# Slot rows of the MoE compared from broadcast places instead of transposed one-hot rows, with the mixers' tails reordered

## The chip, the cores and the metric

The kernel runs on one core of a Trainium2 chip. The metric is the device time of one execution in microseconds (us), the median of several runs. The engines are PE (TensorE; PEld is its weight load), DVE (VectorE), ACT (ScalarE), POOL (GpSimd) and SP (SyncE, which here only issues DMAs).

## The reference

Two layers on one sequence of 256 tokens, 1024 wide, all in float32:

```python
for l in range(2):
    sh1, sc1, g1, sh2, sc2, g2 = split(silu(c) @ ada_w[l] + ada_b[l], 6)
    h = rmsnorm(x, norm_mix_g[l]) * (1 + sc1) + sh1
    pa, pb, pc = split(h @ w_in[l])            # three head groups A, B, C
    mix = concat(oa, ob, oc) @ w_out[l]        # A differential, B sliding window with sinks, C dilated
    x = x + g1 * mix
    h = rmsnorm(x, norm_ffn_g[l]) * (1 + sc2) + sh2
    # router: best of 4 groups, then 2 of its 4 experts, gates sum to the group's weight
    y = sum over 16 experts e: gate[:, e] * ((silu(h @ w_gate[e]) * (h @ w_up[e])) @ w_down[e])
    x = x + g2 * y
return rmsnorm(x, final_norm_g)
```

## The kernel before, in words

Tokens lie on the 128 partitions in two tiles t = 0, 1. All weights, 283 MB, pass once through on-chip memory: SP issues their loads one after the other in a fixed order (`Ring.load`, L154) into a ring of 29 tiles of 512 KB (`big`), with tiles of the pools `k` and `w` lent to it now and then. A tile is loaded again only when its last reader (a PE matmul, or the DVE that splits it) has finished; when SP reaches such a load too early it waits, and every load behind it with it.

PE runs in the order in which the program is written. The orders of DVE, ACT and POOL are set by a scheduler when the kernel is built, and each engine then runs its own list strictly from front to back.

**The mixer** of a layer is written as a list of steps, `MIX`, which ends in `TAIL`. `P..` are the pieces of the input projection and `W.` those of the output projection; weights are split into two fp32r parts for them (cast on ACT, L776; subtraction on DVE, L781) and three matmuls made of each (L724 to L726). `AT, BT, CT` transpose a head group's queries and keys (L809, copies at L1074 on ACT and L1075 on DVE for group C). `AF, BF, CF` make scores (L1081) into one bank of the two-buffer PSUM pool `s` for each half of the heads, read them on DVE (L835, masked maximum, then nm at L839) and take exponentials on ACT (L841). `BV, CV` transpose the probabilities (L809) and copy them out (L866, ACT). Letters `a`, `c`, `d` are chunks of the adaLN products (a: L462, d: L537; a `d` is half of the 16 matmuls that the trace shows for two). Behind each `W` and `P`, `flush` runs work put off until then: among it `ada_columns` (L480), four transposes that turn adaLN rows into columns.

**The MoE** takes the experts in eight pairs j. Each token that chose an expert has a place in it, at most 64 of them, and `pos[:, t, e]` is that place plus one, or 0. One-hot matrices `hot` (tokens by slots) gather the rows of a pair. For the way back the kernel needs the transposed matrix, slots by tokens: `places(j)` makes it. Before pair 0 stand a chain of gates on POOL (L1279 to L1301) and, after the pair's gate products (L1372), `g2` (L568, copied out at L571 and L573). Pair 0's products `up` follow `places(0)` on PE.

Of the kernel before, what the change touches and what calls it, by code (L numbers as in the profile page):

```python
# [17 lines left out]
DEPTH = 2  # L18
# [19 lines left out]

_COLUMNS = (("ID", 128), ("C", KT), ("COLS", (6 * DEPTH + 2 * DEPTH) * KT), ("FREQ", 48), ("PAIR", 2), ("ADD", 2 * DEPTH), ("Z", 128), ("CAUSAL", 128),
            ("CFAR", 128), ("CDIAG", 128), ("IOTA", 64), ("LOW", 16), ("RANK", 4), ("ONES", 1),  # L40
            ("SEL", 20), ("SUBG", DEPTH * 64), ("SINK", DEPTH * 8), ("WR", DEPTH * KT * 20), ("RB", DEPTH * 20),
            ("BAND", 128), ("CAUSAL2", 128))
_AT, NCONST = {}, 0
for _name, _n in _COLUMNS:
# [11 lines left out]

START = ["X c c R c c S00".split(), "S00 S01 X0 X1 a S02 X2 a X3 a a R a".split()]
TAIL = """
CT0 d CT1 d d CF0 AM1 d W0 CF1
BV0 BV1 W1 BV2 BV3 BO0 BV4 W2 BV5 CV0 W3 BO1 CV1 CV2 W4 CO0 W5 W6  # L60
"""
MIX = [("""
P00 c P01 c P10 c c N P11 P02 P03 a a P12 L AT0 P13 a a AT1
P20 AF0 P21 a AF1 P22 a AF2 P23 a a
P30 AV0 P31 AV1 a AO0 BT0 P32 AV2 BT1 AO1 G2 P33 AO2 BF0 a a
P40 P41 BF1 a P42 AM0 P43 BF2 a a a H2 a
""" + TAIL).split(), ("""
P00 P01 P02 P03 P10 P11 AT0 P12 AT1 P13 AF0
P20 AF1 P21 a AF2 P22 P23
P30 AV0 P31 AV1 a AO0 BT0 P32 AV2 BT1 AO1 P33 AO2 BF0 a  # L70
P40 P41 BF1 P42 G2 AM0 P43 BF2 H2
""" + TAIL).split()]


# [6 lines left out]
def laid_out(inputs):  # L81


    t = {n: np.asarray(a) for n, a in inputs.items()}
    i = np.arange(128)[:, None]
    j = np.arange(128)[None, :]
    blob = np.zeros((128, NCONST), np.float32)
    blob[:, _AT["ID"]] = i == j
    blob[:, _AT["CAUSAL"]] = np.where(i >= j, 0.0, -BIG)
    blob[:, _AT["BAND"]] = np.where(j > i, 0.0, -BIG)  # L90

    def mixture(dist):
        n = (((dist >= 0) & (dist <= 128)).astype(int) + ((dist >= 0) & (dist % 4 == 0))
             + ((dist >= 0) & (dist % 16 == 0)))
        return np.where(n > 0, 8.0 * np.log(np.maximum(n, 1)), -BIG)

    blob[:, _AT["CFAR"]] = mixture(128 + i - j)
    blob[:, _AT["CDIAG"]] = mixture(i - j)
    blob[:, _AT["IOTA"]] = np.arange(1, 65)
    blob[:, _AT["LOW"]] = (np.arange(4)[:, None] > np.arange(4)[None, :]).reshape(16)  # L100
    blob[:, _AT["RANK"]] = [3, 2, 1, 0]
    freq = blob[:, _AT["FREQ"]]
    freq[:, 0:32] = (10000.0 ** (-np.arange(0, 64, 2) / 64)).astype(np.float32)
    freq[:, 32:48] = (10000.0 ** (-np.arange(0, 32, 2) / 32)).astype(np.float32)
    blob[:, _AT["ONES"]] = 1.0
    blob[:, _AT["PAIR"]] = i % 64 == 32 * np.arange(2)
    lh = np.arange(2 * DEPTH)
    blob[:, _AT["ADD"]] = (i == 64 + 32 * (lh % 2) + lh // 2) | (i == 32 * (lh % 2) + DEPTH)
    blob[:, _AT["SEL"]] = i % 32 == np.arange(20)
    blob[:, _AT["C"]] = by_partition(t["c"])  # L110
    blob[:, _AT["COLS"]] = by_partition(np.concatenate(
        [t["ada_b"].reshape(6 * DEPTH, D), t["norm_mix_g"], t["norm_ffn_g"]]))
    blob[:, _AT["SUBG"]] = t["diff_subln_g"].reshape(1, -1)
    blob[:, _AT["SINK"]] = t["swa_sinks"].reshape(1, -1)
    wr = np.concatenate([t["router_group_w"], t["router_expert_w"]], axis=2).reshape(DEPTH, KT, 128, 20)
    blob[:, _AT["WR"]] = wr.transpose(2, 0, 1, 3).reshape(128, -1)
    blob[:, _AT["RB"]] = np.concatenate([t["router_group_b"], t["router_expert_b"]], axis=1).reshape(1, -1)
    out = {"first": blob[:, :_AT["Z"].start], "rest": blob[:, _AT["CAUSAL"].start:_AT["CAUSAL2"].start]}
    out["x"] = t["x"]
    out["positions"] = t["positions"].reshape(2, 128).T  # L120
    out["lambdas"] = np.stack([t["diff_lambda_" + n] for n in ("q1", "k1", "q2", "k2")]).reshape(1, -1)
    out["final_norm_g"] = t["final_norm_g"]
    w = t["ada_w"][0, :, :2 * D].reshape(KT, 128, 2, 2, 512)
    out["ada_w_first"] = w.transpose(3, 0, 1, 2, 4).reshape(2, KT, 128, 1024)
    out["ada_w"] = t["ada_w"].reshape(DEPTH, KT, 128, 6 * D)
    w = t["w_in"].reshape(DEPTH, 4, 2, 128, 2304)
    out["w_in"] = w[..., :2048].reshape(DEPTH, 4, 2, 128, 4, 512).transpose(0, 4, 1, 3, 2, 5).reshape(DEPTH, 4, 4, 128, 1024)
    out["w_in_last"] = w[..., 2048:].transpose(0, 1, 3, 2, 4).reshape(DEPTH, 4, 128, 512)
# [71 lines left out]
class Body:  # L200
# [60 lines left out]
    def tables(self, posi):  # L261
        nc, const, cb = self.nc, self.const, self.cb

        posf = const.tile([128, 2], F32, name="posf")
        nc.vector.tensor_copy(posf, posi)
        ang = self.w()[:, 0:96].rearrange("p (t f) -> p t f", t=2)
        for t in range(2):
# [33 lines left out]
    def more_tables(self):  # L301
        nc, const, cb = self.nc, self.const, self.cb
        for l in range(DEPTH):
            nc.vector.tensor_scalar(self.subg[:, l], self.subg[:, l], 1.0 - self.lambda_init(l), None, op0=OP.mult)
        self.sink8 = const.tile([128, DEPTH, 8], F32, name="sink8")
        nc.vector.tensor_scalar(self.sink8, self.sink, 8.0, None, op0=OP.mult)
        self.trib = const.tile([128, 128], BF16, name="trib")
        nc.vector.tensor_scalar(self.trib, cb[:, C_CAUSAL:C_CAUSAL + 128], 0.0, None, op0=OP.is_lt)
        oneb = const.tile([128, 1], BF16, name="oneb")
        nc.vector.tensor_copy(oneb, cb[:, C_ONES:C_ONES + 1])  # L310
        self.oneb = oneb.to_broadcast([128, 128])
        self.ovf = const.tile([128, DEPTH], F32, name="ovf")

        self.beats = const.tile([128, 10, 4, 5], F32, name="beats")
        nc.gpsimd.tensor_copy(self.beats[:, :, :, 4],
                              cb[:, C_RANK:C_RANK + 4].unsqueeze(1).to_broadcast([128, 10, 4]))
# [138 lines left out]
    def ada_unit(self, l, q, i):  # L455
        nc = self.nc
        if i == 0:
            self.q = self.acc.tile([128, 512], F32, name="acc")
        keys = [("ada", l, v, i) for v in (2 * q, 2 * q + 1)]
        w = [self.ring.take(k) for k in keys]  # L460
        for j in range(4):
            nc.tensor.matmul(self.q[32 * j:32 * j + 32, :], lhsT=self.cact[:, i:i + 1].to_broadcast([128, 32]),  # L462
                             rhs=w[j // 2][:, 512 * (j % 2):512 * (j % 2) + 512], start=(i == 0), stop=(i == KT - 1))
        for k in keys:
            self.ring.finish(k)
        if i < KT - 1:
            return
        rows = self.w()
        if q == 0:
            nc.vector.tensor_copy(rows, self.q)  # L470
        else:
            nc.scalar.copy(rows[64:128], self.q[64:128])
            nc.vector.tensor_tensor(out=rows[0:64], in0=self.q[0:64], in1=self.qb[0:64], op=OP.add)
        self.pending.append(lambda: self.pending.append(lambda: self.ada_columns(l, q, rows)))

    def ada_columns(self, l, q, rows):
        nc = self.nc
# [97 lines left out]
    def flush(self):  # L575

        now, self.pending = self.pending, []
        for f in now:
            f()

    def spread(self, l, v):

# [679 lines left out]
    def gates_of_tokens(self, l, dense, lg, l5, rank, og, tl):  # L1262
# [43 lines left out]
        nc.scalar.copy(self.g2rows[0], rows)  # L1306
        nc.vector.tensor_tensor(out=self.g2rows[1], in0=rows, in1=self.g2rows[0].bitcast(F32), op=OP.subtract)

    def one_hot(self, b):

        one = self.w(F32R).rearrange("p (t e s) -> p t e s", t=2, e=4)
        iota = self.cb[:, C_IOTA:C_IOTA + CAP].unsqueeze(1).to_broadcast([128, 4, CAP])
        for t in range(2):
            i = self.nc.vector.tensor_tensor(out=one[:, t], in0=iota, op=OP.is_equal,  # L1314
                                             in1=self.pos[:, t, 4 * b:4 * b + 4].unsqueeze(2).to_broadcast([128, 4, CAP]))
        self.hot[b] = one.rearrange("p t e s -> p t (e s)")
        return i


    def moe(self, l):  # L1320
# [23 lines left out]
        def places(j):  # L1344

            p = self.pt.tile([128, 512], F32, name="t")
            hf = hot[j // 2][:, :, 128 * (j % 2):128 * (j % 2) + 128]
            for t in range(2):
                nc.tensor.transpose(p[:, 128 * t:128 * t + 128], hf[:, t].bitcast(F32), self.ident)  # L1349
            for t in range(2):  # L1350
                nc.tensor.matmul(p[:, 256:288], lhsT=hf[:, t],
                                 rhs=self.ghl[:, t].rearrange("p u e -> p (u e)"), start=(t == 0), stop=(t == 1))
            pt = self.w(F32R)[:, 0:S]
            nc.scalar.copy(pt, p[:, 0:256])
            gs = self.small.tile([128, 1], F32, name="gs")
            for u in range(2):
                e = 2 * j + u
# [148 lines left out]
        for j in range(8):  # L1506
            gates_of(j, (lambda: down_in(j - 1)) if j else None)
            if j == 0:
                self.g2(l)
                g = self.mod[l, 5]  # L1510
            if j:
                parts = down(j - 1)
            places(j)
# [146 lines left out]
```

## Time and profile before

| | |
|---|---|
| median of 3 runs | 746.31 us (746.07 to 747.48) |
| the profiled execution | 746.45 us, its span 744.6 us |
| busy in the span | PE 708.5 us (95%), DVE 343.4 (46%), ACT 213.4 (29%), POOL 62.4 (8%) |
| DMA | 283.63 MB, mean 381 GB/s over the span |
| mean granted TensorE clock | 0.986 of full speed |

The profiled execution is 0.14 us above the median, inside the runs' own spread, so its rows stand for the runs. The 1.85 us between span and time lie around the span in both kernels. Since both PE and DMA are nearly always busy, a share of the whole span says little: which of the two sets the time changes from stage to stage, and must be read stage by stage.

### The profile page before, as it was taken

How to read it: one execution, taken by the hardware profiler on the slowest of the kernel's cores; microseconds unless marked ns; L12 is line 12 of the kernel's file. 1: busy time of each engine (PE TensorE's matmuls, PEld its weight loads, DVE VectorE, ACT ScalarE, POOL GpSimd, SP SyncE). 2: the span in 40 equal slices, each digit the busy share in tenths (PEclk: the TensorE clock that was granted, in tenths of full speed). 3: DMA queues.
4: the chain of work that ended last, by engine and by line, in shares of the span. 5: the costliest groups of instructions: out<-in, count | busy, mean ns of one | idle time of the engine just before them, and what ended most of it. 6: DMA issues, size and time to landing. Idle time of an engine off the chain costs nothing. (4 is left out here: it accounts for less than half of the span.)

```text
span 744.6 us, 10676 instructions
## 1 busy us (share of the span) xinstructions
PE 708.5 (95%) x3790; PEld 369.1 (50%) x3790; DVE 343.4 (46%) x941; ACT 213.4 (29%) x485; POOL 62.4 (8%) x86
## 2 busy tenths in 40 slices
PE   6899998999999999999999999898999999999993
PEld 2565765764353353353347678575435335344341
DVE  4677796364132233133358879737313312332234
ACT  2445445433111110111134555644211011111012
POOL 1011234001000000000001121400100000000001
PEclk9899999899999999999999999999999999999998
DMA  9999999999989999999999996969899999999991
GB/s 352 409 409 407 407 408 409 407 387 408 406 349 409 409 410 408 409 409 410 399 406 409 405 407 224 354 218 405 315 358 403 406 409 409 409 409 409 409 386 65
DMA packets 82457, 283.63 MB, mean 381 GB/s; under 512 B 9166, under 2 KB 9295, under 8 KB 82396
## 3 DMA queue, kind: packets, MB, share of 16 engines
q1 hardware_dynamic: 82186, 282.85, 96.7%
q8 instruction: 32, 0.52, 0.3%
q14 instruction: 29, 0.24, 0.1%
q0 software_dynamic: 64, 0.02, 0.0%
q10 hardware_dynamic: 146, 0.00, 0.0%
HBM read 281.78 MB, written 1.06 MB: 380 GB/s over the span
## 5 line engine op out<-in xcount | busy, mean ns | idle before, releaser
L1372 PE MATMUL s<-big,k 128*64 128x512 f32 x976 | 228.2, 598 | 0.0
L1372 PEld LDWEIGHTS s<-big,k 128*64 128x64 f32 x976 | 67.3, 136 | 118.6 <-issue 103.8
L1424 DVE SCALAR_TENSOR_TENSOR w<-acc,gs,g 128x512 f32<-128x512 f32 x28 | 21.0, 751 | 155.3 <-PE acc L1418 153.8
L1418 PE MATMUL acc<-big,w 128*64 128x512 f32 x384 | 84.4, 592 | 0.0
L781 DVE TENSOR_TENSOR k<-big,k 128x1024 fp32r<-128x1024 f32 (+1 forms) x56 | 66.8, 1201 | 14.3 <-ACT k L776 10.5
L724 PE MATMUL acc<-k 128*128 128x512 f32 (+1 forms) x176 | 69.9, 397 | 2.9 <-ACT k L713 2.0
L725 PE MATMUL acc<-k 128*128 128x512 f32 (+1 forms) x176 | 66.4, 377 | 0.0
L726 PE MATMUL acc<-k 128*128 128x512 f32 (+1 forms) x176 | 66.4, 377 | 0.0
L776 ACT CAST k<-big 128x1024 fp32r<-128x1024 f32 (+1 forms) x56 | 54.1, 983 | 38.9 <-PE acc L725 27.5
L1418 PEld LDWEIGHTS acc<-big,w 128*64 128x64 f32 x384 | 27.6, 137 | 54.8 <-issue 52.5
L1403 DVE TENSOR_TENSOR w<-w,s 128x512 f32<-128x512 f32 x16 | 11.0, 687 | 82.8 <-PE s L1372 82.8
L1428 ACT CAST w<-w 128x512 fp32r<-128x512 f32 x28 | 17.3, 618 | 89.8 <-DVE w L1424 89.8
L724 PEld LDWEIGHTS acc<-k 128*128 128x128 f32 x176 | 33.8, 192 | 17.9 <-issue 6.9
L841 ACT ACTIVATE w<-w,nm 128x128 f32<-128x128 f32 (+1 forms) x80 | 35.4, 444 | 21.4 <-DVE nm L839 21.4
L1338 PEld LDWEIGHTS t<-w,k 128*128 128x128 f32 x256 | 32.8, 190 | 16.3 <-issue 9.9
L1409 ACT COPY w<-t 128x512 f32<-128x512 f32 x16 | 9.3, 584 | 106.4 <-PE t L809 106.4
L1338 PE MATMUL t<-w,k 128*128 128x256 f32 x256 | 37.6, 291 | 1.7 <-DVE w L1314 1.7
L730 ACT ACTIVATE k<-t,mod,mod 128x256 f32<-128x256 f32 x32 | 16.3, 559 | 77.3 <-PE t L1338 77.3
L726 PEld LDWEIGHTS acc<-k 128*128 128x128 f32 x176 | 33.7, 192 | 7.4 <-DVE k L897 1.4
L809 PE MATMUL t<-cb,w 128*128 128x128 f32 x224 | 35.2, 287 | 2.1 <-ACT w L866 1.1
L725 PEld LDWEIGHTS acc<-k 128*128 128x128 f32 x176 | 33.9, 193 | 5.0
L1441 DVE TENSOR_TENSOR x<-x,acc 128x512 f32<-128x512 f32 x56 | 34.9, 683 | 0.2
(272 smaller groups left out, 851.1 us busy)
## 6 DMA issues: line engine op xcount, KB each, us to landing
big<-in_expert_w_up_dram SPq DMA_DIRECT2D x126, 512.0 KB, 10.2
big<-in_expert_w_gate_dram SPq DMA_DIRECT2D x118, 512.0 KB, 10.2
big<-in_expert_w_down_dram SPq DMA_DIRECT2D x108, 512.0 KB, 10.1
big<-in_ada_w_dram SPq DMA_DIRECT2D x80, 512.0 KB, 10.2
big<-in_w_in_dram SPq DMA_DIRECT2D x32, 512.0 KB, 10.2
big<-in_ada_w_first_dram SPq DMA_DIRECT2D x16, 512.0 KB, 10.2
big<-in_w_out_dram SPq DMA_DIRECT2D x16, 512.0 KB, 9.5
w<-in_expert_w_down_dram SPq DMA_DIRECT2D x20, 256.0 KB, 5.9
```

The costliest lines, as they stand in the source:

```text
L724: self.nc.tensor.matmul(p, lhsT=xh, rhs=wh, start=start, stop=False)
L725: self.nc.tensor.matmul(p, lhsT=xh, rhs=wl, start=False, stop=False)
L726: self.nc.tensor.matmul(p, lhsT=xl, rhs=wh, start=False, stop=stop)
L776: nc.scalar.copy(hi, w)
L781: nc.vector.tensor_tensor(out=lo, in0=w, in1=hi.bitcast(F32), op=OP.subtract)
L809: self.nc.tensor.transpose(p[:, i], b, self.ident)
L841: nc.scalar.activation(e[:, h], e[:, h], AF.Exp, bias=nm[:, g:g + 1], scale=scale, accum_out=sm[:, g:g + 1])
L1338: nc.tensor.matmul(p[:, kk], lhsT=part[t][:, 2 * k2 + kk], rhs=one[:, t], start=(n == 0), stop=(n == 3))
L1372: nc.tensor.matmul(store[j][64 * u:64 * u + 64, :], lhsT=x[k // 4][:, k % 4, c:c + 64], rhs=w[u][kk], start=(k == 0), stop=(k == KT - 1))
L1418: nc.tensor.matmul(ps[hf][64 * u:64 * u + 64, :], lhsT=act[j][:, f, 64 * u:64 * u + 64], rhs=w[u][hf], start=(f == 0), stop=(f == 3))
L1424: nc.vector.scalar_tensor_tensor(out=ds[-1], in0=p, scalar=gates[j], in1=g[:, 512 * hf:512 * hf + 512], op0=OP.mult, op1=OP.mult)
L1441: nc.vector.tensor_tensor(out=self.x[t][:, c], in0=self.x[t][:, c], in1=p, op=OP.add)
```

## The change

1. `places(j)`: instead of two transposes of `hot` on PE and a copy on ACT, one bf16 matmul repeats the places of the two experts over 64 partitions each (`halves` picks the two rows, `post` holds the places by experts and tokens), and a comparison on DVE with the column SLOT (the partition's slot plus one) makes the matrix.
2. `places_of_tokens()`, once a layer behind `g2`: POOL clears a tile and copies the places into it, PE transposes it four times, ACT copies it into `post`.
3. The mixers' lists: `CT0`, `CT1` stand behind `P40`, `P41` instead of in the tail; `CF1` stands behind `BV0 BV1`, and one more `d` ahead of `W0`.
4. `ada_columns` of q = 0 (layer 0 alone has one that is put off in this way) runs at the fifth flush instead of the second.
5. The order of the DMAs is the same; one of them, of constants, is one column wider.

```diff
 TAIL = """
-CT0 d CT1 d d CF0 AM1 d W0 CF1
-BV0 BV1 W1 BV2 BV3 BO0 BV4 W2 BV5 CV0 W3 BO1 CV1 CV2 W4 CO0 W5 W6
+d d CF0 AM1 d d W0 BV0 BV1 CF1
+W1 BV2 BV3 BO0 BV4 W2 BV5 CV0 W3 BO1 CV1 CV2 W4 CO0 W5 W6
 """
...
-P40 P41 BF1 P42 G2 AM0 P43 BF2 H2
+P40 CT0 P41 CT1 BF1 P42 G2 AM0 P43 BF2 H2
...
-        self.pending.append(lambda: self.pending.append(lambda: self.ada_columns(l, q, rows)))
+        self.later_on(2 if q else 5, lambda: self.ada_columns(l, q, rows))
...
+    def places_of_tokens(self):
+
+        nc = self.nc
+        x = self.w().rearrange("p (t h c) -> p t h c", t=2, h=2)
+        nc.gpsimd.memset(x, 0.0)
+        for t in range(2):
+            for h in range(2):
+                out = x[:, t, h].rearrange("p (j c) -> p j c", j=4)[:, :, 0:2]
+                nc.gpsimd.tensor_copy(out, self.pos[:, t, 8 * h:8 * h + 8].rearrange("p (j u) -> p j u", j=4))
+        p = self.transposes([x[:, t, h] for h in range(2) for t in range(2)])
+        nc.scalar.copy(self.post, p)
...
-            for t in range(2):
-                nc.tensor.transpose(p[:, 128 * t:128 * t + 128], hf[:, t].bitcast(F32), self.ident)
+            r = slice(32 * (j % 4), 32 * (j % 4) + 32)
+            nc.tensor.matmul(p[:, 0:256], lhsT=self.halves[r], rhs=self.post[r, j // 4], start=True, stop=True)
...
-            nc.scalar.copy(pt, p[:, 0:256])
+            nc.vector.tensor_scalar(pt, p[:, 0:256], self.cb[:, _AT["SLOT"]], None, op0=OP.is_equal)
...
                 self.g2(l)
                 g = self.mod[l, 5]
+                self.places_of_tokens()
```

Lines of the changed kernel are higher by 10 in the mixer's middle and end (L835 becomes L845, L1081 becomes L1091), by 22 in the first half of the MoE (L1372 becomes L1394).

Three places show how instructions move. First PE in layer 1, from the last scores of group B (the first row) to the first matmul of `W0` (the last); L809 there is CT0, CT1 and AM1 in turn, L537 the `d`, and the second L1081 is CF0. Before:

```order
L1081 MATMUL s<-w,k 128x256 x4
L809 MATMUL t<-cb,w 128x128 x4
L537 MATMUL acc<-big,cb 32x512 x4
L809 MATMUL t<-cb,w 128x128 x4
L537 MATMUL acc<-big,cb 32x512 x8
L1081 MATMUL s<-w 128x128 x4
L809 MATMUL t<-cb,w 128x128 x2
L537 MATMUL acc<-big,cb 32x512 x4
L724 MATMUL acc<-k,w 128x512
```

After, where CT0 and CT1 have gone forward into the projection:

```order
L1091 MATMUL s<-w,k 128x256 x4
L543 MATMUL acc<-big,cb 32x512 x8
L1091 MATMUL s<-w 128x128 x4
L819 MATMUL t<-cb,w 128x128 x2
L543 MATMUL acc<-big,cb 32x512 x8
L734 MATMUL acc<-k,w 128x512
```

Between the scores of B and those of C stand no transposes any more, only two `d`; the other two stand together behind AM1.

Second, DVE in the same place, where a `d` may run on PE: L835 with an operand `s` are the reads of B's last scores (two for each of the two banks), L781 the splits of `w_out` for `W0`, L1075 the copies of C's keys, L1058 is AM0's. Before:

```order
L1048 TENSOR_TENSOR w<-w,rya 128x256
L781 TENSOR_TENSOR k<-big,k 128x1024
L1058 TENSOR_TENSOR w<-t,w 128x2x128
L1049 TENSOR_TENSOR w<-w,cb 128x256
L835 ISA w,mx<-s,cb 128x256
L835 ISA mx 128x1
L835 ISA w,mx<-s,cb 128x256
...
L835 ISA w,mx<-s,cb 128x256
...
L781 TENSOR_TENSOR k<-big,k 128x1024
...
L1075 COPY w<-t 128x2x128
...
L781 TENSOR_TENSOR k<-big,k 128x1024
L1075 COPY w<-t 128x2x128
```

After, from the same norm of group A's output on:

```order
L1085 COPY w<-t 128x2x128
...
L1058 TENSOR_TENSOR w<-w,rya 128x256
...
L791 TENSOR_TENSOR k<-big,k 128x1024
...
L1059 TENSOR_TENSOR w<-w,cb 128x256
L791 TENSOR_TENSOR k<-big,k 128x1024
L1068 TENSOR_TENSOR w<-t,w 128x2x128
L845 ISA w,mx<-s,cb 128x256
...
L845 ISA w,mx<-s,cb 128x256
...
L791 TENSOR_TENSOR k<-big,k 128x1024
L845 ISA w,mx<-s,cb 128x256
...
L845 ISA w,mx<-s,cb 128x256
```

One copy of C's keys (the other stands further ahead) and a second split now stand ahead of the first read, and a third split stands between the two banks.

Third, ACT in the tail of layer 0: L841 with 128x256 are the exponentials of CF1, L866 the copies of BV0 and those behind it. Before:

```order
L1057 CAST w<-t 128x2x128
L841 ACTIVATE w,sm<-w,nm 128x128 x2
L776 CAST k<-big 128x1024
L841 ACTIVATE w,sm<-w,nm 128x128 x2
L776 CAST k<-big 128x1024
L841 ACTIVATE w,sm<-w,nm 128x256 x4
L866 COPY w<-t 128x512 x4
```

After:

```order
L1067 CAST w<-t 128x2x128
L851 ACTIVATE w,sm<-w,nm 128x128 x4
L786 CAST k<-big 128x1024 x2
L876 COPY w<-t 128x512 x3
L851 ACTIVATE w,sm<-w,nm 128x256 x4
L876 COPY w<-t 128x512
```

The first copies stand ahead of CF1's exponentials now.

## Rows read from the trace of the kernel before

**Rows 1.** Windows by stage: us, then length and busy us by engine, granted clock (PEclk), DMA share, GB/s.
```profile
140.00:230.00 90.00, 87.45 (x495) 44.69 (x495) 33.53 (x85) 21.88 (x45) 3.09 (x12) 1.00 0.99 391
230.00:440.00 210.00, 207.33 (x999) 99.45 (x996) 94.25 (x215) 53.19 (x112) 9.77 (x8) 1.00 1.03 408
...
560.00:724.00 164.00, 164.00 (x802) 68.54 (x800) 48.02 (x91) 22.51 (x43) 1.48 (x2) 1.00 1.03 407
```

**Rows 2.** Windows inside 140 to 230, same columns, where DMA falls short.
```profile
152.00:162.00 10.00, 9.73 (x58) 6.75 (x61) 7.01 (x16) 3.58 (x10) 0.00 (x0) 1.00 1.00 367
204.00:208.00 4.00, 4.00 (x21) 1.45 (x21) 2.01 (x5) 1.21 (x3) 0.00 (x0) 1.00 0.43 152
```

**Rows 3.** Waits of SP's queue between 140 and 230: total, times, longest (us).
```profile
SPq L154 <- PE s L1372: 31.5, 18, 5.4
```

**Rows 4.** PE's timeline at the start of layer 1's products: start, us, instruction.
```profile
381.46 2.05 PE L462 MATMUL acc<-big,cb 128*32 128x512 f32 x8
```

**Rows 5.** PE's timeline, tail of layer 0; brackets hold idle time before and its releaser.
```profile
128.84 0.66 PE L480 MATMUL t<-cb,w 128*128 128x128 f32 x4 [1.96 <-ACT w L866]
```

**Rows 6.** ACT's timeline in the tail of layer 0.
```profile
126.24 0.51 ACT L841 ACTIVATE w<-w,nm 128x256 f32<-128x256 f32 x1 [4.39 <-DVE nm L839]
...
128.22 1.04 ACT L866 COPY w<-t 128x512 f32<-128x512 f32 x2
```

**Rows 7.** Windows around these, columns as in rows 1.
```profile
20.00:24.00 4.00, 1.95 (x8) 1.58 (x8) 3.78 (x10) 2.10 (x4) 0.00 (x0) 0.55 1.03 410
128.00:132.00 4.00, 3.16 (x16) 2.73 (x16) 1.50 (x5) 1.85 (x5) 2.04 (x2) 0.70 1.03 411
132.00:136.00 4.00, 4.00 (x22) 2.79 (x22) 0.42 (x1) 1.17 (x2) 0.00 (x0) 0.50 1.03 409
136.00:140.00 4.00, 4.00 (x22) 3.28 (x22) 2.65 (x4) 3.95 (x5) 0.00 (x0) 0.95 1.03 410
468.00:472.00 4.00, 2.67 (x26) 0.98 (x18) 4.00 (x15) 3.17 (x10) 0.00 (x0) 1.00 0.96 293
```

**Rows 8.** PE's timeline, tail of layer 1.
```profile
467.19 0.63 PE L809 MATMUL t<-cb,w 128*128 128x128 f32 x4 [0.76 <-DVE w L1058]
467.75 1.92 PE L537 MATMUL acc<-big,cb 128*32 128x512 f32 x16
471.00 0.71 PE L1081 MATMUL s<-w 64*128 64x128 f32 x8 [1.33 <-DVE w L1075]
...
473.01 0.50 PE L724 MATMUL acc<-k,w 128*128 128x512 f32 x1
...
482.60 1.09 PE L809 MATMUL t<-cb,w 128*128 128x128 f32 x8 [0.46 <-ACT w L866]
```

**Rows 9.** DVE's timeline, tail of layer 1.
```profile
464.62 2.09 DVE L781 TENSOR_TENSOR k<-big,k 128x1024 fp32r<-128x1024 f32 x1
...
467.81 0.41 DVE L835 CUSTOM_DVE_ANT_0 w<-s,cb 128x256 f32<-128x256 f32 x1
...
469.26 1.21 DVE L781 TENSOR_TENSOR k<-big,k 128x1024 fp32r<-128x1024 f32 x1
...
470.54 0.41 DVE L1075 COPY w<-t 128x256 f32<-128x256 f32 x1
```

**Rows 10.** POOL's timeline, tail of layer 1.
```profile
464.58 3.02 POOL L857 TENSOR_TENSOR w<-w,rc 128x512 f32<-128x512 f32 x2 [8.42 <-ACT k L776]
```

**Rows 11.** PE's timeline in layer 1, pair 0's `places`.
```profile
531.83 0.38 PE L1349 MATMUL t<-cb,w 128*128 128x128 f32 x2
...
532.27 4.08 PE L1372 MATMUL s<-big,k 128*64 128x512 f32 x18
```

**Rows 12.** ACT's timeline there.
```profile
532.78 0.58 ACT L571 COPY g<-acc 128x512 f32<-128x512 f32 x1
533.25 0.39 ACT L1354 CAST w<-t 128x256 fp32r<-128x256 f32 x1
```

**Rows 13.** POOL's timeline there, the last of its gate chain.
```profile
527.58 0.25 POOL L1301 TENSOR_TENSOR ghl<-gate,ghl 128x32 fp32r<-128x32 f32 x1
```

More of the change, by code (lines that the diff above doesn't have):

```diff
@@ L40 @@
             ("CFAR", 128), ("CDIAG", 128), ("IOTA", 64), ("LOW", 16), ("RANK", 4), ("ONES", 1),
-            ("SEL", 20), ("SUBG", DEPTH * 64), ("SINK", DEPTH * 8), ("WR", DEPTH * KT * 20), ("RB", DEPTH * 20),
+            ("SEL", 20), ("SLOT", 1), ("SUBG", DEPTH * 64), ("SINK", DEPTH * 8), ("WR", DEPTH * KT * 20), ("RB", DEPTH * 20),
             ("BAND", 128), ("CAUSAL2", 128))
@@ L65 @@
 P30 AV0 P31 AV1 a AO0 BT0 P32 AV2 BT1 AO1 G2 P33 AO2 BF0 a a
-P40 P41 BF1 a P42 AM0 P43 BF2 a a a H2 a
+P40 CT0 P41 CT1 BF1 a P42 AM0 P43 BF2 a a a H2 a
 """ + TAIL).split(), ("""
@@ L109, in laid_out @@
     blob[:, _AT["SEL"]] = i % 32 == np.arange(20)
+    blob[:, _AT["SLOT"]] = i % 64 + 1
     blob[:, _AT["C"]] = by_partition(t["c"])
@@ L262, in tables @@
         nc, const, cb = self.nc, self.const, self.cb
-        posf = const.tile([128, 2], F32, name="posf")
+        posf = self.w()[:, 0:2]
         nc.vector.tensor_copy(posf, posi)
@@ L308, in more_tables @@
         nc.vector.tensor_scalar(self.trib, cb[:, C_CAUSAL:C_CAUSAL + 128], 0.0, None, op0=OP.is_lt)
+        self.halves = const.tile([128, 128], BF16, name="halves")
+        nc.gpsimd.tensor_copy(self.halves.rearrange("p (u s) -> p u s", u=2),
+                              cb[:, C_SEL:C_SEL + 2].unsqueeze(2).to_broadcast([128, 2, 64]))
+        self.post = const.tile([128, 2, S], BF16, name="post")
         oneb = const.tile([128, 1], BF16, name="oneb")
@@ L579, in flush, with later_on @@
             f()
+    def later_on(self, n, f):
+        self.pending.append(f if n == 1 else lambda: self.later_on(n - 1, f))
     def spread(self, l, v):
```

## Prediction

> **What bounds the kernel now.** I read first the windows by stage, because PE and DMA are both nearly always busy and only a stage tells which of them sets the time. Where DMA moves some 408 GB/s it can do no more in this kernel; where it moves less while weights are still to come, SP is held up. Between 230 and 440 us and between 560 and 724 us DMA is full (408 and 407 GB/s), between 140 and 230 it is not (391) [rows 1]. Missing there is 90 x (408 - 391) / 408 = 3.75 us of transfer, and two windows hold nearly all of it: 10 x (408 - 367) / 408 = 1.0 us at 152 to 162, and 4 x (408 - 152) / 408 = 2.5 us at 204 to 208 [rows 2]. The waits of SP's queue say why: its loads wait for PE to finish with a tile, the longest for 5.4 us behind an expert product [rows 3]. There the ring is full and PE is late.
>
> Next I looked where that loss is paid. In the MoE of layer 0 PE is faster than the transfers, the ring drains, and at the start of layer 1 PE waits for data: eight adaLN matmuls take 2.05 us [rows 4], where sixteen with their data there take 1.92 [rows 8]. So up to there DMA sets the time, and a loss made good at 152 to 208 comes through whole. In the mixer that follows PE sets it: the ring is full again, and SP waits for PE and DVE to give tiles back. From 560 DMA is full to 724 us, and what PE saves there is hidden; but what makes PE late before 560 holds SP up and moves the whole end.
>
> So the change has to be judged at four places: the tail of layer 0, `places(0)` of layer 0 (both by what they do to the two windows of lost DMA), the tail of layer 1 and `places(0)` of layer 1 (both by PE's own time).
>
> **Tail of layer 0.** PE waits 1.96 us for an ACT copy before `ada_columns` [rows 5]. ACT's timeline shows the copies queued behind four exponentials of CF1, which had themselves waited 4.39 us for DVE [rows 6]. Behind that wait the granted clock falls to its lower level: 0.70, 0.50 and 0.95 of full speed in three windows [rows 7], which is (0.30 + 0.50 + 0.05) x 4 / 0.5 = 6.8 us at 1.2 instead of 2.4 GHz, and with PE busy 3.4 us of work lost. The change takes away both reasons: ACT has the copies ahead of CF1's exponentials, and `ada_columns` comes three outputs later. I take the whole 1.96 + 3.4 = 5.4 us as PE's lead at 140. The bounds are 0 (another wait stands there, for POOL's normalised probabilities or for DVE, and the clock falls again) and 5.4.
>
> **`places(0)`, both layers.** Before, PE makes the two transposes at 531.83 and is at `up` at 532.27 [rows 11]. Now PE needs `post`, and `post` is copied by ACT. On ACT that copy stands behind the copy L571, in the place of L1354, which starts at 533.25 [rows 12]. At the 0.58 us of L571, also 128x512 from PSUM [rows 12], it ends at 533.83. The one matmul and the two gate matmuls are estimated at 0.45 us, the 0.44 that the old group took from start to start [rows 11], so `up` starts at 534.3 instead of 532.27: +2.0 us a layer. What is late next is every expert product of pair 0 and the loads that wait for its tiles. The new work of POOL ahead of it should be hidden: the gate chain ends at 527.83 [rows 13]; the trace shows no 128x512 memset of POOL, so I bound a clear and four small copies by five times the 0.25 us of its last row below and by 3.0 us (two whole multiplications of 128x512 [rows 10]) above, which gives 529.1 to 530.8, ahead of PE's 531.83 in both. PE's four transposes lie inside its wait. The bounds of the term are 0.2 (ACT free at once) and 2.0, and more only if the clock falls in this 1.5 us of waiting.
>
> In layer 0 the same 2.0 is taken from the lead: 5.4 - 2.0 = 3.4 us at 206. The first window lies ahead of `places(0)` (182) and gets the full lead; in the second the 5.4 us wait shrinks to 2.0, less than the 5.4 - 2.5 = 2.9 us of it that the transfers in flight cover. Both losses go: **-3.5 us** (bounds 0 and -3.75).
>
> **Tail of layer 1.** Here CF0 stands on PE behind B's last scores and must have both banks of `s`, which DVE frees by reading them. Before, the four reads start at 467.81 and are over when the next split starts at 469.26; CF0 waits until 471.00 for the copy of C's keys, 1.33 us, and CT1 ahead of it waits 0.76 [rows 8, 9]. DVE is busy for all 4.00 of the 4 us from 468 [rows 7], so whatever its list puts ahead of the reads makes them late. The list after has both key copies (0.41 each) and one split (1.21) more ahead of the first read, and another split between the two banks [rows 9]. That is 467.81 + 2.0 = 469.8 for the first read, 0.7 for two of them, 1.2 for the split, 0.7 for the last two: CF0 has its second bank at 472.4, 1.4 us later than before. From CF0 to `W0` it was 2.01 us with one `d` [rows 8]; now there are two, at 0.96 each: `W0` at 472.4 + 2.97 = 475.4 instead of 473.01, +2.4. The 0.46 that PE waits for an ACT copy at 482.60 [rows 8] is then no longer a wait: **+1.9 us** net. Bounds: if DVE has the reads done in time, nothing waits and the 2.1 us of waiting are won (-2.1); above, +1.9 and a fall of the clock.
>
> That fall is the term I had to choose. With CT0 and CT1 gone ahead and their wait with them, PE ends its two `d` at 469.67 - 0.96 - 0.76 = 467.95 and then has only half of CF0 until 472.4: about 4.4 us near idle. Waits of 0.76 and 1.33 left the clock at 1.00 [rows 7, 8], the wait of 1.96 was followed by 6.8 us at the lower level [rows 5, 7], and PE's idle half of 20 to 24 by 0.55 [rows 7]. The new wait is longer than either of the harmful ones, so I take the fall, at the 3.4 us of layer 0: **+3.4**.
>
> The Trainium skill bears on this: "TensorE: Matmul & The Clock Gate", in Part 1 on the clock gate and in "Loop structure matters more than you think", says that TensorE falls to half its clock after standing idle and that long waits between groups of matmuls make them run cold. By it the sum has the 3.4 us; by the row at 468 alone, where 1.33 us of waiting left the clock whole, it does not, and the two sums are those of the first two cases below. The trace bears the rule out where PE waited 1.96 us, and not at 1.33.
>
> A split beside POOL's multiplications took 2.09 us, and 1.21 without them [rows 9, 10]. The skill's "GPSIMD Engine Reference", Specifications, says that POOL shares its ways to memory with VectorE. By that page a second split beside POOL would add the same 0.9 us to the sum; I don't count it, since POOL has as much to do there as before.
>
> **Later pairs.** One matmul for two transposes saves at most the 0.38 us that the two show [rows 11]; by the estimate of half, 0.2, pair 1 gives 0.2 before 560 and the six later ones nothing, since DMA is full there. The comparison moves from ACT to DVE, which is busy 48 of the 164 us after 560 [rows 1]; its result is wanted only at the weighting behind the down products. Without that cover it would cost one instruction like the 0.41 us copy [rows 9] a pair.
>
> **The sum.** -3.5 + 1.9 + 3.4 + 2.0 - 0.2 = +3.6 us on 746.45; the median is 0.14 lower, which I leave to the range: **750.0 us**. A measurement of this kernel can tell some 0.2%, 1.5 us, from no change.
>
> **The rivals.**
> - *The tail waits, the clock holds.* PE still has parts of CF0 in between, and the lower level may not come. Then the 3.4 falls away: +0.2, 746.6 us, no change that can be told.
> - *The tail works (faster).* One mechanism: DVE reaches B's reads in time, because its splits of `w_out` run without POOL beside them (1.21 for 2.09) and the list ahead of them is done sooner. It decides at 469.7, where PE would start CF0 without a wait: each read done later costs PE directly. In full it gives -3.5 - 2.1 + 2.0 - 0.2 = -3.8, 742.6 us. For it speaks that PE's tail has less that waits for DVE between the scores; against it the 4.00 of 4 us [rows 7].
> - *Layer 0 gains nothing.* BV0 comes ahead of CF1 and may meet POOL, or the clock falls there anyway. Then -3.5 is 0: 753.5 us.
> - *It is hidden.* `post` comes early and the tails differ by less than a us: 745 to 747.5.
>
> **How the numbers follow.** Chances: forecast 0.42, clock holds 0.20, tail works 0.25, nothing in layer 0 0.06, hidden 0.07. The forecast's own range is 748.0 to 752.5 (its bank reads 1 us sooner, its `places(0)` cheaper; or the clock falling also at a `places(0)`). The whole range goes from 743.0, in the middle of the faster case, to 752.5: left out are about half of that case and the case above. Slower by over 0.2%: 0.42 + 0.06 and a part of the second, 0.50. Same: the rest of the second and the hidden case, 0.23. Faster: 0.27.
>
> **What would show it.** After the change the trace should have no wait before L486 near 128 and a clock of 1.00 there; DMA at 408 at 204 to 208; in layer 1 a wait of PE for DVE's reads (L845) before CF0, some 4 us, with `W0` about 2.4 us later against the start of `P43`, and lowered clock behind it; in both layers a wait of 1.5 us for ACT before the matmul with `post`. I am wrong if CF0 starts at once, or if `W0` of layer 1 runs at full clock.

## The result

The changed kernel takes 756.26 us in the median (752.6 to 758.33), the one before 746.89 beside it: a ratio of 1.0109, interval 1.0073 to 1.0146, so 0.7 to 1.5% slower. Slower was forecast, by 3.6 us; it is about 8 by the ratio (the medians lie 9.4 apart, the profiled executions 8.7).

The profiled execution took 755.15 us, its span 753.4 us, against 746.45 and 744.6. Its page, the busy part (columns as before: busy us, share of the span, instructions):

```profile
span 753.4 us, 10663 instructions
PE 712.6 (95%) x3782; PEld 368.6 (49%) x3782; DVE 348.9 (46%) x957; ACT 210.4 (28%) x471; POOL 64.1 (9%) x97
```

PE's sum is 4.1 us larger for slightly fewer instructions, and the rest of the 8.8 is waiting. Its waits between 40 and 754 us (what for: total, times, longest) name them:

```profile
PE t L1371 <- ACT post L1329: 2.9, 2, 1.5
PE s L1091 <- DVE mx L845: 2.6, 2, 1.3
PE t L819 <- DVE w L1085: 1.9, 1, 1.9
...
PE t L819 <- DVE mod L561: 0.9, 1, 0.9
...
PE acc L734 <- DVE w L552: 0.6, 1, 0.6
```

The first is `post` at pair 0 of both layers; the second is CF0 of layer 1, the third the two transposes AM0 of layer 1 (group A's output, right behind P42); the last two are layer 0's tail. Before, the long waits that the changed kernel no longer has were L480 in layer 0 [rows 5] and the two in layer 1's tail [rows 8]. Windows of [rows 1, 2] again, and six at falls of the clock:

```profile
120.00:124.00 4.00, 3.15 (x21) 2.45 (x21) 3.61 (x6) 0.44 (x1) 1.72 (x2) 0.84 1.03 408
124.00:128.00 4.00, 4.00 (x17) 2.85 (x17) 0.32 (x1) 1.07 (x2) 0.00 (x0) 0.73 1.03 410
140.00:230.00 90.00, 85.95 (x488) 43.55 (x489) 33.62 (x89) 20.46 (x41) 3.75 (x17) 1.00 0.99 387
152.00:162.00 10.00, 9.38 (x84) 6.31 (x82) 8.43 (x24) 4.08 (x11) 0.26 (x1) 1.00 1.03 376
204.00:208.00 4.00, 4.00 (x21) 1.56 (x21) 2.99 (x7) 1.24 (x2) 0.00 (x0) 1.00 0.31 107
472.00:476.00 4.00, 2.66 (x18) 1.36 (x22) 3.33 (x20) 2.05 (x9) 0.00 (x0) 0.79 0.97 351
476.00:480.00 4.00, 4.00 (x24) 1.74 (x14) 2.33 (x6) 1.94 (x11) 3.21 (x4) 0.78 1.02 412
536.00:540.00 4.00, 2.53 (x13) 1.37 (x14) 1.40 (x4) 2.53 (x4) 0.00 (x0) 0.90 0.87 309
540.00:544.00 4.00, 4.00 (x16) 1.30 (x14) 0.00 (x0) 0.00 (x0) 0.00 (x0) 0.68 0.43 161
560.00:724.00 164.00, 164.00 (x793) 67.22 (x791) 50.40 (x97) 21.59 (x38) 1.48 (x2) 1.00 1.01 400
```

The clock falls in three places, once in each tail and once behind the wait for `post` in layer 1. A fall costs PE up to (1 - clock) x length: (0.16 + 0.27) x 4 = 1.7 us in layer 0's tail, (0.21 + 0.22) x 4 = 1.7 in layer 1's, and (0.10 + 0.32) x 4 = 1.7 at pair 0. And DMA does not come back at 140 to 230: it moves 387 GB/s instead of 391; the window at 152 has 376 instead of 367, but the one at 204 has 107 instead of 152.

Rows of PE give the rest. Layer 1's tail and pair 0 (start, us, instruction, idle before and its releaser):

```profile
465.87 0.44 PE L819 MATMUL t<-cb,w 128*128 128x128 f32 x2 [1.89 <-DVE w L1085]
...
471.87 0.48 PE L1091 MATMUL s<-w 64*128 64x128 f32 x2 [1.22 <-DVE mx L845]
473.69 0.71 PE L1091 MATMUL s<-w 64*128 64x128 f32 x6 [1.34 <-DVE mx L845]
...
478.16 0.50 PE L734 MATMUL acc<-k,w 128*128 128x512 f32 x1
...
536.52 0.60 PE L819 MATMUL t<-cb,w 128*128 128x128 f32 x4
538.59 0.26 PE L1371 MATMUL t<-post,halves 32*128 32x256 bf16 x1 [1.47 <-ACT post L1329]
...
539.11 5.35 PE L1394 MATMUL s<-big,k 128*64 128x512 f32 x16
```

The sum from such rows: the input projection of layer 1 starts at 395.90 instead of 394.93, **+1.0** (layer 0); `W0` at 478.16 instead of 473.01 [rows 8], +5.15, and the router some 4.7 later than before, so **+3.7** in the tail; `up` of pair 0 at 539.11 instead of 532.27 [rows 11], +6.84, so **+2.15** at `places(0)`; then **+1.7** by the fall behind it and **+0.3** later. Together 8.85, and the spans differ by 8.8. Three falls of 1.7 us stand in this sum, and one of 3.4 in the kernel before [rows 7]. Since falls come elsewhere in another execution (e9 below), the split holds for these two executions.

### The profile page after: what moved, and what is told of

Read it like the earlier page. It is cut to its first block, busy times and chain, and to the rows that moved or that the text cites. A ratio compares the mean times of both kernels' runs of the same rounds, so it can differ in the third digit from the quotient of the medians.

```text
span 753.4 us, 10663 instructions
## 1 busy us (share of the span) xinstructions
PE 712.6 (95%) x3782; PEld 368.6 (49%) x3782; DVE 348.9 (46%) x957; ACT 210.4 (28%) x471; POOL 64.1 (9%) x97
## 3 DMA queue, kind: packets, MB, share of 16 engines
HBM read 281.78 MB, written 1.06 MB: 375 GB/s over the span
## 5 line engine op out<-in xcount | busy, mean ns | idle before, releaser
L1394 PE MATMUL s<-big,k 128*64 128x512 f32 x976 | 229.9, 601 | 0.0
L1394 PEld LDWEIGHTS s<-big,k 128*64 128x64 f32 x976 | 67.8, 137 | 119.9 <-issue 106.8
```

The costliest lines, as they stand in the source:

```text
L1394: nc.tensor.matmul(store[j][64 * u:64 * u + 64, :], lhsT=x[k // 4][:, k % 4, c:c + 64], rhs=w[u][kk], start=(k == 0), stop=(k == KT - 1))
```

## The experiments

My theory after the result: three costs that add up, (a) PE's wait for `post` on ACT in both layers, (b) the new waits for DVE in layer 1's tail, (c) falls of the clock behind such waits; and layer 0's gain, which is small. The rivals: that lists and places only hurt together, or that the time goes elsewhere (DVE's comparisons, POOL's new work). The ratios in the headings below are to the kernel before, timed beside each, with 95% intervals.

**e1_lists_columns**: lists and `ada_columns` without the new places. **1.0031 (1.0008 to 1.0053).** Its edit, against the kernel before:

```diff
-CT0 d CT1 d d CF0 AM1 d W0 CF1
-BV0 BV1 W1 BV2 BV3 BO0 BV4 W2 BV5 CV0 W3 BO1 CV1 CV2 W4 CO0 W5 W6
+d d CF0 AM1 d d W0 BV0 BV1 CF1
+W1 BV2 BV3 BO0 BV4 W2 BV5 CV0 W3 BO1 CV1 CV2 W4 CO0 W5 W6
...
-P40 P41 BF1 P42 G2 AM0 P43 BF2 H2
+P40 CT0 P41 CT1 BF1 P42 G2 AM0 P43 BF2 H2
...
-        self.pending.append(lambda: self.pending.append(lambda: self.ada_columns(l, q, rows)))
+        self.later_on(2 if q else 5, lambda: self.ada_columns(l, q, rows))
```

> The kernel before with the reordered lists of both mixers and the later ada_columns, and with the old places. If the three parts add up one by one, layer 0 reaches its router about 1.5 us earlier (as after the whole change), which gives back up to 1.5 us of lost DMA, and layer 1's tail costs the 3.7 us it costs after the whole change: PE waits about 1.9 us for the key copy L1075 between the two halves of P42, and in two pieces of 1.2 to 1.3 us for DVE's score reads before CF0, with a fall of the clock behind it. Together about +2 us (748.5). Rival: the 8.8 us come mostly from places, and this kernel is level with the one before or faster (745 to 747).

749.34 us beside 747.46. The waits stand as forecast (1.9 for the key copy, which stands before AM0, and 2.6 before CF0). The fall of the clock that was forecast behind them does not come: in the profiled execution no clock falls in either tail. PE reaches the router at 159.24 instead of 162.08, and DMA moves 404 GB/s at 140 to 230. So without `places(0)` in its way a lead of layer 0 does come back as transfers; where this lead comes from is read under e6. The lists cost about 2 us on balance.

**e2_places**: the new places alone. **1.0075 (1.0049 to 1.0100).** The edit is the change without its parts 3 and 4:

```diff
-d d CF0 AM1 d d W0 BV0 BV1 CF1
+CT0 d CT1 d d CF0 AM1 d W0 CF1
...
-        self.later_on(2 if q else 5, lambda: self.ada_columns(l, q, rows))
+        self.pending.append(lambda: self.pending.append(lambda: self.ada_columns(l, q, rows)))
```

> The kernel before with the new places and post alone; lists and ada_columns as before. If the wait for post is paid in both layers: 1.5 us of waiting for ACT and 0.6 of transposes at pair 0 of each layer, in layer 0 as DMA lost at 204 to 208 (2.5 us before, about 4.5 now), in layer 1 directly (+2.1), and up to 1.7 more where the clock falls behind the wait: +4 to +6 us (750 to 752). Rival: the wait for post is hidden where layer 0's tail is as before, and the cost lies in the lists: +1 us or less.

753.62 us beside 747.46, 5.6 us more by the ratio: inside the forecast difference. With e1 that is 0.31 + 0.75 = 1.06%, and the whole change has 1.09. The parts add up within their intervals, and some two thirds of the loss is places. DMA falls to 378 GB/s at 140 to 230 here.

**e3_columns**: `ada_columns` later, alone. **0.9982 (0.9963 to 1.0000).**

```diff
-        self.pending.append(lambda: self.pending.append(lambda: self.ada_columns(l, q, rows)))
+        self.later_on(2 if q else 5, lambda: self.ada_columns(l, q, rows))
```

> The kernel before with the later ada_columns alone. By the prediction's reading the 1.96 us wait before L480 goes. My reading now: the next transposes of probabilities (L809) need the same ACT copies, so they wait there instead, about 1.5 us, and the clock falls there all the same: within 1 us of before. Rival (the prediction's step): both the wait and the 3.4 us at the lower clock go, and DMA lost at 204 to 208 comes back, -2.5 to -3.5 us (743 to 744).

746.86 us. Where PE waited before L480 it now waits before the next instruction that needs a buffer of the PSUM pool `t` (timeline of PE in layer 0's tail; L607 is the router's bias product, in this kernel's numbering):

```profile
128.43 0.40 PE L607 MATMUL t<-w,ones 128*128 128x20 f32 x2 [1.98 <-ACT w L870]
```

1.98 us for 1.96: moving the waiting instruction away saves nothing of the wait, since ACT's late copies hold the buffer. The gain, if there is one (the interval ends at no change), is not this wait. One half of my reading missed in this execution: the clock did not fall behind the wait (1.00 at 120 to 140, where the kernel before has 0.83). It fell later, in the routers and in layer 1's tail.

**e4_up_first**: the whole change with `places(0)` behind `up` of pair 0. **1.0034 (1.0015 to 1.0052).**

```diff
-            places(j)
+            if j:
+                places(j)
             for hh in range(4):
                 first("up", U, j, hh)
+            if j == 0:
+                places(j)
```

> The kernel after the change with places(0) behind the four up products of pair 0 on PE instead of ahead of them; nothing else moves. If the wait for post is a cost of its own, PE no longer waits for ACT there, and no half clock follows: some 2 us (layer 0, as DMA won back) and 2 to 4 us (layer 1) less than after the change, 749 to 752 where that kernel has 755 to 756. Rival: the time is set by DMA or by the tail alone, and moving the wait away changes nothing (755 to 756).

750.43 us: no wait for `post` is left in the trace, and of the 1.1% two thirds are gone; what remains is what e1 has. The rival is out: the two intervals do not meet.

**e5_places_up_first**: the same edit on the kernel before with the new places alone. **1.0033 (1.0008 to 1.0057).**

```diff
-            places(j)
+            if j:
+                places(j)
...
+            if j == 0:
+                places(j)
```

> The kernel before with the new places alone, but places(0) behind the four up products of pair 0. If the whole cost of the new places (+6 us in the run with places alone) is PE's wait for post and what follows from it, this kernel is level with the one before: four transposes more a layer (0.6 us), 0.2 less a pair: between -1 and +1.5 us. Rival: the comparison on DVE or POOL's new work costs too, and 2 us or more remain.

751.04 us beside 748.94. My range ended at 1.5, so this is a miss, by a little: of e2's loss more than half goes with the wait (by the medians; the two intervals overlap a little), but some 2 us seem to stay. Two pairs of runs bear on the same rest: e4 and e1 differ by 0.03%, e8 and e6 (below) by 0.24%, all within their intervals. The four transposes are in PE's way once no wait covers them: 0.52 us a layer from their start to that of `up` in this trace, which would be 1.0 of it. The rest isn't told apart from nothing.

**e6_lists_in_0**: reordered list in layer 0 only, `ada_columns` later, old places. **0.9981 (0.9959 to 1.0002).** Against the kernel before (not shown here: the later `ada_columns`, as in e3):

```diff
+TAIL0 = """
+d d CF0 AM1 d d W0 BV0 BV1 CF1
+W1 BV2 BV3 BO0 BV4 W2 BV5 CV0 W3 BO1 CV1 CV2 W4 CO0 W5 W6
...
-P40 P41 BF1 a P42 AM0 P43 BF2 a a a H2 a
-""" + TAIL).split(), ("""
+P40 CT0 P41 CT1 BF1 a P42 AM0 P43 BF2 a a a H2 a
+""" + TAIL0).split(), ("""
```

> The kernel before with the reordered list in layer 0 only and the later ada_columns; layer 1's list and places as before. If the lists win in layer 0 (2.3 us at the first scores of layer 1 in the run with both lists) and lose in layer 1, this one is 1.5 to 2.5 us faster than before (744.5 to 746). Rival: layer 0's list wins nothing, its lead lay in a clock that happened not to fall in that execution, and this one is level with before.

746.81 us beside 748.94, just short of the forecast gain. Against e1 (layer 1's list is the only difference) it is 0.5% better, so layer 1's list costs some 3.7 us, 1.4 to 6 if the two intervals are put together. By the times it stays open whether layer 0's list wins anything: the interval reaches no change, and e3 without that list has the same ratio.

The traces say more. From the first matmul of P40 to the first of the router PE does the same work in layer 0 with either list. Its first and last row in this run and in e3:

```profile
98.12 0.39 PE L732 MATMUL acc<-k 128*128 128x256 f32 x1
...
161.66 1.06 PE L1204 MATMUL s<-w,wrs 128*32 128x128 f32 x32
```

```profile
98.18 0.39 PE L728 MATMUL acc<-k 128*128 128x256 f32 x1
...
159.11 1.06 PE L1200 MATMUL s<-w,wrs 128*32 128x128 f32 x32
```

| list of layer 0 | runs | clock, 120 to 140 | P40 to router, us |
|---|---|---|---|
| old | before, e5 | 0.83 | 63.5, 63.7 |
| old | e2 | 0.91 | 62.7 |
| old | e3 | 1.00 | 60.9 |
| new | e6 | 0.83 | 63.5 |
| new | after, e9 | 0.91 | 62.1, 62.1 |
| new | e1, e4, e7, e8, e10 | 1.00 | 60.6 each |

At the same clock the new list wins 0 to 0.6 us. What differs by up to 3 us is the clock, and it differs from execution to execution with either list. Whether the new list makes falls rarer is not shown by so few executions.

**e7_filled**: the whole change, with useless matmuls ahead of the one with `post`, whose result nobody reads. **1.0063 (1.0041 to 1.0086).**

```diff
+            if j == 0:
+                for _ in range(12):
+                    nc.tensor.matmul(p[:, 288:512], lhsT=self.add[:, 0:1].to_broadcast([128, 128]),
+                                     rhs=self.g2rows[0][:, 0:224], start=True, stop=True)
             nc.tensor.matmul(p[:, 0:256], lhsT=self.halves[r], rhs=self.post[r, j // 4], start=True, stop=True)
```

> The kernel after the change, with twelve matmuls of 224 columns on PE, whose result nobody reads, ahead of the matmul with post of pair 0: PE does useless work (some 1.2 us) in place of most of its 1.5 us wait. If the clock falls because PE stands idle there, it stays at 1.00 behind the wait, and the time is some 1 to 2 us below that of the kernel after (754 to 755.5 for 756), with up of pair 0 starting no earlier. Rival: the clock falls for another reason (or not more often there than elsewhere) and nothing changes, or the matmuls themselves cost time.

752.91 us, a little below the forecast range. In layer 1 `g2` and `up` of pair 0 start 3.6 us apart both here and after the change, so the wait is as long as ever; PE only does something in it. The windows at the two waits, in layer 0 and layer 1:

```profile
182.00:190.00 8.00, 8.00 (x39) 2.94 (x40) 1.04 (x4) 0.00 (x0) 0.00 (x0) 1.00 1.03 410
536.00:544.00 8.00, 7.86 (x42) 3.41 (x43) 0.71 (x3) 1.09 (x3) 0.00 (x0) 1.00 0.87 314
```

The clock stays at 1.00. The time is 0.2 to 0.5% below that of the whole change (1.0087 and 1.0109 in two sets of runs), which the overlapping intervals do not tell from nothing. One trace does not show either that the fall needs the idle time, but all traces together speak for it. Four of them (after, e2, e9, e11) have PE idle for 1.47 us before the matmul with `post`, in both layers: behind six of these eight waits the clock fell. It never fell there in the six traces in which PE works through the wait (e7), waits half as long (e10) or does not wait (e4, e5, e8, e12), twelve places in all.

**e8_lists_in_0_up_first**: e6 and the new places with `places(0)` behind `up`. **1.0005 (0.9979 to 1.0032).**

```diff
-""" + TAIL).split(), ("""
+""" + TAIL0).split(), ("""
...
-            places(j)
+            if j:
+                places(j)
...
+            if j == 0:
+                places(j)
```

> The new places with places(0) behind up, the reordered list in layer 0 only, the later ada_columns: the parts of the change that cost nothing by the runs so far. If the parts add up, 1.5 to 3 us faster than before (744 to 746). Rival: the lead of layer 0 is not passed on when pair 0 also carries four more transposes, and it is level with before.

747.7 us: level, not faster. The forecast gain missed. Whether the new places' transposes take back what e6 may win is not shown: both intervals reach no change.

**e9_after_again**: the changed kernel unchanged. **1.0087 (1.0059 to 1.0116).**

> The kernel after the change, unchanged, beside the next three on one chip, and a second execution's profile. The waits must stand where they stood (1.5 us for post twice, 1.9 for the key copy, 1.2 and 1.3 before CF0), since they follow from the instructions' order; the falls of the clock may stand elsewhere. Some 754 to 757 us. If instead every execution has the same falls, chance has no part in them.

754.81 us. The waits for `post` and the key copy are the same to a tenth; of the two before CF0 only one is left, 1.13 us, so that part of the forecast missed. The clock falls elsewhere; two windows of this execution, and PE's rows in layer 1's tail:

```profile
182.00:190.00 8.00, 7.90 (x31) 2.68 (x32) 0.71 (x3) 0.04 (x1) 0.00 (x0) 0.79 1.01 391
466.00:472.00 6.00, 4.88 (x30) 3.97 (x34) 6.00 (x18) 5.34 (x14) 3.02 (x2) 0.72 0.61 196
```

```profile
464.63 0.60 PE L486 MATMUL t<-cb,w 128*128 128x128 f32 x4
...
474.94 0.71 PE L1091 MATMUL s<-w 64*128 64x128 f32 x6 [1.13 <-DVE mx L845]
...
477.81 0.50 PE L734 MATMUL acc<-k,w 128*128 128x512 f32 x1
```

Now it falls behind `post` in layer 0 too (1.00 there in the first profile: 182 to 190), and in layer 1 behind the 1.9 us wait instead of behind CF0's. Each again is 1.7 us by the windows (0.21 x 8 and 0.28 x 6), but the one in layer 1's tail costs no time here: from L486 to `W0` are 13.18 us, as in e1 and e7, whose clock holds there; after the change they were 14.78. The fall ahead of CF0 went into the wait for DVE's reads. So waits of 0.8 us (layer 0's tail) to 2 us bring a fall in some executions and not in others, and what a fall costs hangs on what PE waits for next.

**e10_post_on_dve**: the whole change, `post` copied by DVE. **1.0045 (1.0030 to 1.0061).**

```diff
-        nc.scalar.copy(self.post, p)
+        nc.vector.tensor_copy(self.post, p)
```

> The kernel after the change with post copied by DVE instead of ACT; all else the same. If PE waits for post because it is queued on ACT behind the table load, SiLU and the copy of L577, the wait shrinks from 1.5 us to about 0.7 (one copy of 128x512 behind PE's transposes) in both layers, and the falls of the clock behind it become rarer: 2 to 4 us less than after (752 to 754). Rival: the wait follows from the chain places, transposes, copy itself, whichever engine copies, and the time stays.

751.02 us. PE's timeline at pair 0 of layer 1:

```profile
536.45 0.26 PE L1371 MATMUL t<-post,halves 32*128 32x256 bf16 x1 [0.78 <-DVE post L1329]
```

Half the wait is gone, and with it 0.4 to 0.6% of the time (a little below the forecast range). That is more than the 0.7 us a layer that the wait shrank; no fall stands behind either wait in this profile. That half of the wait was ACT's queue; the other 0.78 us stay with the chain of transposes and copy.

**e11_keys_on_act**: the whole change, the copy of C's keys on ACT. **1.0060 (1.0038 to 1.0082).**

```diff
-            nc.vector.tensor_copy(T["kc"][:, :, blk(t)], p[:, 2:4])
+            nc.scalar.copy(T["kc"][:, :, blk(t)], p[:, 2:4])
```

> The kernel after the change with the copy of C's keys (L1085) on ACT instead of DVE. If layer 1's tail is late because these copies queue on a DVE that has no time to spare, the 1.9 us wait in P42 goes, the reads of B's scores come some 0.8 us sooner on DVE's list, and no split stands between the two banks any more, so that the waits before CF0 shrink from 2.6 to about 1: 2 to 3.5 us less than after (752.5 to 754). Rival: ACT is as busy there and the wait changes only its engine (755 to 757).

752.04 us, 0.3 to 0.5% below the whole change, with intervals that overlap. PE's waits in layer 1's tail:

```profile
464.97 0.44 PE L819 MATMUL t<-cb,w 128*128 128x128 f32 x2 [1.18 <-ACT w L1085]
...
470.16 0.48 PE L1091 MATMUL s<-w 64*128 64x128 f32 x2 [0.41 <-DVE mx L845]
470.85 0.71 PE L1091 MATMUL s<-w 64*128 64x128 f32 x6 [0.20 <-DVE mx L845]
```

CF0's 2.6 us are 0.6. The wait for the key copy only shrinks to 1.2, now for ACT, so here the rival is half right. The edit acts in layer 0's tail too: P40 to router takes 59.3 us with no fall, where the other runs with the new list and no fall take 60.6. So the gain need not be layer 1's tail alone.

**e12_mended**: e11 with `places(0)` behind `up`. **1.0009 (0.9997 to 1.0022).**

```diff
-            nc.vector.tensor_copy(T["kc"][:, :, blk(t)], p[:, 2:4])
+            nc.scalar.copy(T["kc"][:, :, blk(t)], p[:, 2:4])
...
-            places(j)
+            if j:
+                places(j)
...
+            if j == 0:
+                places(j)
```

> The kernel after the change with both mended: places(0) behind up, and the copy of C's keys on ACT; the reordered lists in both layers. If the two waits and what they pull behind them are all the cost, what is left is layer 0's gain and the cheaper places of the later pairs: 745 to 748, level with before or 1 to 2 us faster. Rival: some 2 us of cost stay elsewhere, as in the run with places behind up on the old lists: 749 to 750.

748.61 us beside 747.32, a little above the range. With the one wait gone and the other shorter the change is level with the kernel before; no gain is left over, and the later pairs' places are not cheaper, as is read below. No version is faster than the kernel before beyond its interval.

## Why the prediction was wrong

The direction was right, the size was 2.2 times too small, and the time lies outside the range.

- **Tail of layer 0, the step that failed: "The change takes away both reasons", with its lead of 5.4 us at 140.** PE reached the router 1.5 us ahead. First before, then after:

```profile
123.45 0.66 PE L809 MATMUL t<-cb,w 128*128 128x128 f32 x4 [0.20 <-DVE mod L555]
...
162.08 1.06 PE L1196 MATMUL s<-w,wrs 128*32 128x128 f32 x32
```

```profile
119.85 0.50 PE L734 MATMUL acc<-k,w 128*128 128x512 f32 x1 [0.58 <-DVE w L552]
...
122.94 1.11 PE L819 MATMUL t<-cb,w 128*128 128x128 f32 x4 [0.85 <-DVE mod L561]
...
130.50 0.66 PE L819 MATMUL t<-cb,w 128*128 128x128 f32 x4 [0.38 <-DVE rbias L616]
...
133.77 0.50 PE L734 MATMUL acc<-k 128*128 128x512 f32 x1 [0.58 <-ACT k L906]
...
160.59 1.06 PE L1206 MATMUL s<-w,wrs 128*32 128x128 f32 x32
```

  The waiting did not go: 0.58 + 0.85 + 0.38 + 0.58 = 2.39 us in place of 0.20 + 1.96 = 2.16 [rows 5]. Of the two edits the later `ada_columns` takes away no wait (e3: 1.98 for 1.96, before the next user of the same PSUM pool). The reordered list has ACT's copies in time, but brings BV1 the wait for L561, which CF1 used to cover, `W0` the one for L552, and two more. And the clock still falls, for 1.7 instead of 3.4: that difference is the lead. The 3.4 was no price of the wait before L480: behind it the clock lost 3.4 us of PE's work in two traces, 1.7 in one and nothing in one (table under e6), and at the same clock the new list wins 0 to 0.6 us. The sign named for this step came true (no wait before L486, clock 1.00 at 128 to 132) without the gain, because wait and fall now stand elsewhere. The bound "another wait stands there" was written down and given 0.06. With 1.5 instead of 5.4 nothing was left behind `places(0)`: its +2.0 made PE late at 206, so the loss of DMA grew. The term of -3.5 was +1.0. That is 4.5 of the 5.2 us by which the sum was short in the profiled execution; the fall behind `post` (+1.7), the dearer later part (+0.5), `places(0)` itself (+0.15) and the cheaper tail of layer 1 (-1.6) make up the rest.
- **`places(0)`:** +2.0 forecast, 2.15 measured in layer 1, by the mechanism named (ACT's queue: `post` copied at 537.94 to 538.54, behind L577). POOL was hidden as estimated: its clear took 0.52 and its four copies 0.57, done at 533.99, ahead of PE's transposes at 536.52. What was left out of the sum is the clock's fall behind this wait, 1.7 us here, named only as an upper bound. The count under e7 speaks for idleness as its reason.
- **Tail of layer 1:** +1.9 of waiting and +3.4 for the clock forecast, +3.7 measured: waits of 1.89 + 1.22 + 1.34 in place of 0.76 + 1.33 + 0.46 [rows 8] are +1.9, and the fall costs 1.7. The reads came between splits as read from the order, CF0's second bank at 473.69 - 1.0 of late start = 472.7 against 472.4. But part of the waiting stands elsewhere: CT1's PSUM tile is held by the key copy, queued on DVE at 465.40, and the transposes AM0, behind P42, wait for that tile. e11 shows CF0's waits to be DVE's queue, and 0.7 of the 1.9 us before AM0. The idle time was thus in pieces, not one of 4.4 us, and the fall half as dear. By its own sign the prediction is wrong here too: `W0` ran at full clock (1.00 at 478 to 480); the fall lay ahead of it, on the two `d` (3.28 us for 1.92).
- **The rule of the clock.** The fall came in layer 1's tail (0.79 and 0.78 at 472 to 480), and at 1.7 us; the 3.4 us had been taken from the one larger fall before [rows 7]. The Trainium skill's "TensorE: Matmul & The Clock Gate", Part 1, says that TensorE falls to half its clock after standing idle. The traces agree that falls stand behind waits, but only behind some of them: six of the eight for `post`, and none of two in e7, where PE was kept busy.
- **Later pairs** gained nothing: from `up` of pair 0 to the end PE lost 2.0 us, 1.7 by the fall and 0.3 beside it. The term of -0.2 was mis-sized, since the new matmul is not cheaper than the two transposes. The last pair, before and after:

```profile
711.46 0.44 PE L1349 MATMUL t<-cb,w 128*128 128x128 f32 x2
711.66 0.38 PE L1351 MATMUL t<-ghl,w 128*128 128x32 f32 x2
711.96 7.09 PE L1372 MATMUL s<-big,k 128*64 128x512 f32 x32
```

```profile
720.23 0.28 PE L1371 MATMUL t<-post,halves 32*128 32x256 bf16 x1
720.44 0.40 PE L1373 MATMUL t<-ghl,w 128*128 128x32 f32 x2
720.77 7.09 PE L1394 MATMUL s<-big,k 128*64 128x512 f32 x32
```

  From `places` to `up` PE takes 0.54 us instead of 0.50. That a saving there would be hidden by DMA, as the prediction says, no run shows: PE is busy 164.00 of 164 us behind 560 in both kernels and waits for nothing from 580 to 724.

The rivals: the tail did not work (against 0.25), and the case without a gain in layer 0, named with 753.5 us, is the one that came, with a fall of the clock behind `post` on top of it. One of the two reasons given for that case, that the clock falls there anyway, is what the trace shows; the case had a chance of 0.06.

## What to carry to other kernels

When a wait is taken away by moving the instruction that shows it, look for what holds the resource: the next user of the same buffer inherits the wait. A value that an engine's queue delivers late is best asked for late: the same four products ahead of `places(0)` made two thirds of the loss disappear. On PE an idle stretch of 0.8 to 2 us has to be priced with the chance of a lower clock behind it, which here cost up to as much as the wait. And a fall that one execution shows is not the price of the wait ahead of it: the same wait, profiled in four runs, came with 3.4, 1.7 and no loss.

## What was not expected of the hardware

Falls of the clock came in steps of one size: 1.7 us of PE's work each (in the profile of the kernel before, twice that in one go; in e9's layer 1 at no cost in time), and in different places in two executions of the same kernel: at 122, 474 and 539 us in one, at 122, 183, 467 and 538 in the other. They also came behind waits that the kernel before has too: e7 shows one in layer 0's router, where PE's longest single wait is 0.8 us:

```profile
164.00:168.00 4.00, 3.08 (x14) 2.60 (x14) 3.66 (x11) 0.35 (x1) 0.00 (x0) 0.70 1.02 419
```

Most of the spread of one kernel's times over more than 5 us goes with the clock: after the change the run of 758.33 us has a mean granted clock of 0.978 and that of 752.6 one of 0.985, which is 16.6 and 11.3 us lost, 5.3 of the 5.7 between them. That is why differences of a us or two could not be settled by few runs.
